# Two-layer hybrid decoder: the row sums of the later modulation vectors by 32x32 turns on VectorE, their running sums pinned in program order

## The chip, the core and the metric

One of the cores of a Trainium2 chip runs the whole program; the other cores have no part in it. The metric is the device time of one execution in microseconds (us). Each kernel is run several times; one further execution is taken by the hardware profiler, and all views of the profile are of that one execution. In the profile PE is TensorE (PEld its weight loads), DVE is VectorE, ACT is ScalarE, POOL is GpSimd, and SP issues most of the transfers. L391 is line 391 of the kernel.

## What is computed

The reference is a decoder trunk of two layers over 512 positions and 2048 features, in float32. Layer 0 is differential attention, layer 1 is forgetting attention that reads keys and values shared from the output of layer 0. Ahead of each layer, and of the shared keys and values, the input is scaled and shifted by vectors that come from the conditioning `c`; the mixer's output is multiplied by a third such vector.

```python
c_act = jax.nn.silu(c)
for l in range(DEPTH):
    mod = c_act @ w_mod[l] + b_mod[l]
    shift, scale, gate = jnp.split(mod, 3, axis=-1)
    h = x * (1.0 + scale[:, None]) + shift[:, None]
    ...
    x = layer_norm(DN_ALPHA * x + gate[:, None] * y, ln_g[l], ln_b[l])
...
mod = c_act @ w_mod_kv + b_mod_kv
shift, scale = jnp.split(mod, 2, axis=-1)
hk = x * (1.0 + scale[:, None]) + shift[:, None]
```

So eight vectors of 2048 elements are needed, each one row `c_act` times a 2048x2048 matrix plus a bias. Two of them (shift and scale of layer 0) are needed before anything else. The other six, the later modulation, are what the change is about: the gate of layer 0, shift and scale of the shared keys and values, and shift, scale and gate of layer 1.

## The kernel before

**Large products.** Every projection is a product of 512 positions with a weight matrix, in float32 precision from three products in the faster type float32r: each operand is split into a high part (a copy on ScalarE) and a low part (a subtraction on VectorE), and `products` (L171) issues high*high, high*low and low*high, each 128x128 by 128x512. A weight matrix streams through `WeightStream`: a stage `wst` of two 128x512 tiles is loaded on the SP queue, `whi` is cast on ScalarE (L93) and `wlo` subtracted on VectorE (L94), three of each ahead at most. `group` (L306) runs the eight stages of one job over four accumulators, one burst of six products for each stage and accumulator. After each burst `tick` (L290) issues at most one waiting piece of attention from the list `pieces` and a number `bg` of background steps.

**Order of the jobs.** A hand-written start computes the first projections of heads 0 and 1. Then follow the query-key and value-gate groups of heads 2 to 7, with the attention of the head before (`attention_a`, L683) spread over them as pieces, then the output projection of layer 0 in four jobs (`out_projection`, L884), the shared values and keys (four groups each), eight groups of layer 1 with its attention, and its output projection.

**The later modulation before.** `mod_stream` (L355) is a generator of background steps. For each of 24 segments (a vector's 512 columns) it takes the 16 row blocks of the matrix: it loads them (tile `ms`, 512 KB with two row blocks in stage A, 256 KB with one in stage B, where the first 64 go to free tiles `msk`), and each step adds one block, times the column of `cact` that belongs to it, to a 128x512 accumulator `macc` (L389 for the first block, L391 for the rest). Stage A has 16 segments (256 steps) and two `ms` tiles; its steps are issued by the groups of heads 3 to 7 (45 steps a head) and by the first job of the output projection (one after each of its 32 bursts). Stage B has eight segments (128 steps) during the groups of shared values and keys.

What is left of a segment is a sum over the 128 partitions. `mod_row` (L401) does it on TensorE: `macc` is split into `mhi` and `mlo` (L168, L169), two products with a matrix of ones (L411, L412) give 128 equal rows of sums in the one bank `tr`, which attention's turns use as well; VectorE adds the bias to one of these rows (L413, tile `mrow`), and the row goes to a DRAM row that later stages read (`gate_dram`, `mod_dram`). The first half is issued with step 1 of the next segment, the second with step 5.

**Who reads the results.** `out_projection` broadcasts the gate row. `open_n` (L913), called by the evacuation of the first accumulator in the first job of the output projection, runs out the background, then `fold` (L931) brings the shift and scale of the shared keys and values into columns by one turn on TensorE (L934); only behind it, on VectorE, come the evacuations of that job (`ztmp`, L899). Another `fold`, for layer 1, stands in the third group of shared keys.

**What sets the order.** Each engine runs its own instructions strictly in the order in which they stand. That order is made when the program is built: a scheduler takes instructions by priority and by its own idea of when inputs are there, so a step whose inputs it takes for ready can stand earlier on VectorE than where the program issued it. Only the start's VectorE work is kept as written. In the program before, 240 VectorE instructions stand ahead of the first query split of head 2, and 12 of them are running sums of the modulation.

Of the kernel before, what the change touches and what calls it, by code (L numbers as in the profile page):

```python
# [2 lines left out]

# [6 lines left out]
F32 = mybir.dt.float32  # L10
F32R = mybir.dt.float32r
I32 = mybir.dt.int32
AF = mybir.ActivationFunctionType
ALU = mybir.AluOpType

P = 128
D = 2048
# [92 lines left out]
def tile_yoco(  # L110
# [23 lines left out]
    nc = tc.nc  # L134
    V, S, PE, G = nc.vector, nc.scalar, nc.tensor, nc.gpsimd
# [6 lines left out]
    const = ctx.enter_context(tc.tile_pool(name="const", bufs=1))  # L142
# [12 lines left out]
    def acc_bank(name="acc"):  # L155
        return ps.tile([P, 512], F32, name=name, tag="acc", bufs=4)
# [4 lines left out]
    def tr_bank(name="tr"):  # L161
        return ps.tile([P, 512], F32, name=name, tag="tr", bufs=1)
# [4 lines left out]
    def split(hi, lo, src):  # L167
        S.copy(hi, src)  # L168
        V.tensor_tensor(lo, src, hi.bitcast(F32), op=ALU.subtract)  # L169
# [8 lines left out]
    ident = const.tile([P, P], F32, name="ident")  # L178
    make_identity(nc, ident)
    ones = const.tile([P, P], F32, name="ones")  # L180
    G.memset(ones, 1.0)
    mask = const.tile([P, 512], F32, name="mask")
    G.memset(mask, 0.0)
    G.affine_select(
# [14 lines left out]
    pt = tr_bank()  # L199
    PE.transpose(pt[:, 0:KT], crow, ident[0:KT, 0:KT])  # L200
    V.tensor_copy(ccol, pt[:, 0:KT])
    cact = const.tile([P, KT], F32, name="cact")
# [4 lines left out]
    pt = tr_bank()  # L207
# [147 lines left out]
    def mod_stream(segs, new_stage, new_acc, nk, deep=0, new_deep=None):  # L355

        todo = [(i, r) for i in range(len(segs)) for r in range(KT // nk)]
        loaded = {}  # L360
        summed = []

        def load(k):
            i, r = todo[k]
            src, col, _ = segs[i]
            t = new_deep() if k < deep else new_stage()
            rows = src[nk * r * P : nk * (r + 1) * P, col : col + 512]
            nc.sync.dma_start(t, rows.rearrange("(k p) n -> p k n", p=P) if nk > 1 else rows)
            loaded[k] = t

        def load_upto(k):
            n = len(loads)
            while n < len(todo) and n <= (k + 7 if n < deep else k + 2 // nk):
                load(n)
                loads.append(n)
                n += 1

        loads = []
        load_upto(-1)
        for k, (i, r) in enumerate(todo):  # L380
            load_upto(k)
            if r == 0:
                acc = new_acc()
            t = loaded.pop(k)
            for kk in range(nk):
                kt = nk * r + kk
                w = t[:, kk, :] if nk > 1 else t
                if kt == 0:
                    V.tensor_scalar(acc, w, cact[:, 0:1], None, op0=ALU.mult)  # L389
                else:  # L390
                    V.scalar_tensor_tensor(acc, w, cact[:, kt : kt + 1], acc, op0=ALU.mult, op1=ALU.add)  # L391
                if kt == KT - 1:
                    summed.append(segs[i][2](acc))
                if kt in (1, 5) and summed:
                    if next(summed[0], None) is None:
                        summed.pop()
                yield
        for _ in summed[0]:
            yield

    def mod_row(pool, ones_r, dst, bias, one):  # L401

        def steps(acc):
            hi = pool.tile([P, 512], F32R, name="mhi", tag="mhi", bufs=1)
            lo = pool.tile([P, 512], F32R, name="mlo", tag="mlo", bufs=1)
            split(hi, lo, acc)
            row = pool.tile([1, 512], F32, name="mrow", tag="mrow", bufs=1)
            nc.sync.dma_start(row, bias.rearrange("(o n) -> o n", o=1))
            yield True
            pt = tr_bank()  # L410
            PE.matmul(pt, ones_r, hi, start=True, stop=False)  # L411
            PE.matmul(pt, ones_r, lo, start=False, stop=True)  # L412
            V.scalar_tensor_tensor(row, pt[0:1, :], one, row, op0=ALU.add, op1=ALU.add)  # L413
            nc.sync.dma_start(dst, row)
        return steps


# [4 lines left out]
    with tc.tile_pool(name="start", bufs=2, reuse_waits="tile") as sp, tc.manual_schedule(engines={ET.DVE}):  # L422
# [44 lines left out]
        def mod_steps():  # L467
            for n, (i, k, nr) in enumerate(tiles):
                k0, nk = sets[i]
                load_mods(n + NBUF)  # L470
                if k >= KT - on_pe(i):
                    continue
                if k == 0:
                    accs[i] = sp.tile([P, 2, 2 * P], F32, name="sacc", tag="sacc", bufs=2)
                acc = accs[i][:, :, : nk * P]
                for kq in range(nr):
                    w, sc = loaded[i, k][:, kq, :, :], cact[:, k + kq : k + kq + 1]
                    if k + kq == 0:
                        V.tensor_scalar(acc, w, sc, None, op0=ALU.mult)
                    else:  # L480
                        V.scalar_tensor_tensor(acc, w, sc, acc, op0=ALU.mult, op1=ALU.add)  # L481
                    yield i
# [3 lines left out]
        steps = mod_steps()  # L486
# [46 lines left out]
        acc = {}  # L533
# [96 lines left out]
    actx = ExitStack()  # L630
    ap = actx.enter_context(tc.tile_pool(name="ap", bufs=1, reuse_waits="tile"))
    segs = []
    ones_a = ap.tile([P, P], F32R, name="ones_a")
    S.copy(ones_a, ones)
    for dst, src, col, bias, one in (
        (gate_dram[0], w_mod[0], 2 * D, b_mod[0], 0.0),
        (mod_dram[0][0:1, :], kv_w_mod, 0, kv_b_mod, 0.0),
        (mod_dram[0][1:2, :], kv_w_mod, D, kv_b_mod, 1.0),
        (mod_dram[1][0:1, :], w_mod[1], 0, b_mod[1], 0.0),
    ):  # L640
        for f0 in range(0, D, 512):
            cs = slice(col + f0, col + f0 + 512)
            segs.append((src, col + f0, mod_row(ap, ones_a, dst[:, f0 : f0 + 512], bias[cs], one)))
    background = mod_stream(
        segs,
        lambda: ap.tile([P, 2, 512], F32, name="ms", tag="ms", bufs=2),
# [342 lines left out]
    npool, n, nstats = zp  # L989
# [81 lines left out]
    acc = [acc_bank() for _ in range(TB)]  # L1071
    held = {}
    for i, (half, s) in enumerate(lag):
# [7 lines left out]
        hi, lo = held[s]  # L1081
        for b in (2 * half, 2 * half + 1):
            bs = slice(b * P, (b + 1) * P)
            for kq in range(2):
                kt = 2 * s + kq
# [4 lines left out]
            ws.advance(ws.where[id(vj[0]), s] + 4)  # L1090
    forget = [forget_logits(q) for q in range(4)] + [None, forget_sums] + [None] * 8 + [columns_of_f]
    pieces.extend(forget)
    ones_b = npool.tile([P, P], F32R, name="ones_b")
    S.copy(ones_b, ones)
    segs = []
    for dst, col, one in ((mod_dram[1][1:2, :], D, 1.0), (gate_dram[1], 2 * D, 0.0)):
        for f0 in range(0, D, 512):
            cs = slice(col + f0, col + f0 + 512)
            segs.append((w_mod[1], col + f0, mod_row(npool, ones_b, dst[:, f0 : f0 + 512], b_mod[1, cs], one)))
    background = mod_stream(  # L1100
        segs,
        lambda: npool.tile([P, 512], F32, name="ms", tag="ms", bufs=3),
# [243 lines left out]
```

## Time and profile before

| what | value |
|---|---|
| median of 3 runs | 2009.19 us (2004.58 to 2010.02) |
| the profiled execution, device time | 2010.56 us |
| its span (first to last instruction) | 2008.7 us, granted TensorE clock 0.995 |
| ScalarE, VectorE, GpSimd: busy share of the span | 36%, 66%, 0% |
| bytes moved by transfers, mean rate | 353.79 MB, 176 GB/s |
| running sums L391, all forms | 360 instructions, 0.75 us each |

The profiled execution is 1.4 us above the median, inside the spread of the three runs. Busy time of PE is the time in which at least one matmul is under way; matmuls overlap, so the time that a further matmul costs is the distance between starts and not its duration.

### The profile page before, as it was taken

To read this page: it belongs to the slowest core of one execution; us is meant where nothing else is said; L and a number is where in the kernel's file an instruction comes from. 1 tells how busy PE (TensorE), PEld (TensorE's weight loads), DVE (VectorE), ACT (ScalarE), POOL (GpSimd) and SP (SyncE) were. 2 spreads that over 40 slices of the span, in tenths; PEclk is the share of its full clock that TensorE was granted. 3 is DMA by queue.
4 is the path that set the end of the run, shared out by engine and by line. 5 is a ranking of instruction groups with operands and counts; after the bars stand their busy time and mean duration, and the time that the engine had idled before them with its cause. 6 is when DMAs were issued, how large, how long until landed. Compare 5 with 4: busy or idle time off the path is not lost.

```text
span 2008.7 us, 25012 instructions
## 1 busy us (share of the span) xinstructions
PE 1964.6 (98%) x9115; PEld 1627.1 (81%) x9115; DVE 1335.3 (66%) x2436; ACT 725.6 (36%) x1235; POOL 2.2 (0%) x10
## 2 busy tenths in 40 slices
PE   5999999999999999999999999999999999999996
PEld 4888878888888888788888888888888888888885
DVE  6887865677777777853576666635455555576578
ACT  2432445333333334431263222224343434353232
POOL 0000000000000000000000000000000000000000
PEclk8999999999999999999999999999999999999998
DMA  9994742375757676452346787634323232333664
GB/s 338 348 314 147 237 157 78 111 228 182 226 182 229 191 223 209 161 166 95 118 144 223 234 275 260 224 95 131 100 90 105 95 105 90 104 123 104 215 210 178
DMA packets 263095, 353.79 MB, mean 176 GB/s; under 512 B 18022, under 2 KB 162556, under 8 KB 262204
## 3 DMA queue, kind: packets, MB, share of 16 engines
q1 hardware_dynamic: 260592, 347.99, 53.2%
q10 hardware_dynamic: 2380, 4.21, 0.6%
q8 instruction: 71, 1.16, 0.2%
q14 instruction: 52, 0.43, 0.1%
HBM read 339.47 MB, written 12.66 MB: 175 GB/s over the span
## 4 chain that ended last, share of the span: by engine, by line
PE 87%; DVE 6%; DMA 4%; issue 1%; SPq 1%; ACT 0%; DVEq 0%; ACTq 0%
PE acc L173 25%; PE acc L174 25%; PE acc L175 25%; DMA ms<-in_w_mod_dram 3%; PE sc L173 2%; PE sc L174 2%; PE sc L175 2%; DVE wlo L94 1%; PE o L175 1%; PE o L173 1%; PE o L174 1%; DVE macc L391 1%; PE tr L1203 1%; DMA sms<-in_w_mod_dram 1%; SPq L454 0%
## 5 line engine op out<-in xcount | busy, mean ns | idle before, releaser
L94 DVE TENSOR_TENSOR wlo<-wst,whi 128x1024 fp32r<-128x1024 f32 (+2 forms) x338 | 403.4, 1196 | 278.9 <-ACT whi L93 276.9
L93 ACT CAST whi<-wst 128x1024 fp32r<-128x1024 f32 (+2 forms) x338 | 348.5, 1032 | 640.8 <-PE acc L175 327.5
L173 PE MATMUL acc<-whi,hh 128*128 128x512 f32 x1244 | 488.6, 396 | 1.7 <-DVE sg L680 1.7
L174 PE MATMUL acc<-wlo,hh 128*128 128x512 f32 x1244 | 485.3, 390 | 0.8 <-DVE wlo L94 0.8
L175 PE MATMUL acc<-whi,hl 128*128 128x512 f32 x1244 | 485.0, 390 | 0.0
L173 PE MATMUL acc<-hh,whi 128*128 128x512 f32 x1184 | 470.4, 397 | 0.9 <-DVE part L561 0.5
L174 PE MATMUL acc<-hl,whi 128*128 128x512 f32 x1184 | 462.3, 390 | 0.0
L175 PE MATMUL acc<-hh,wlo 128*128 128x512 f32 x1184 | 462.2, 390 | 0.0
L391 DVE SCALAR_TENSOR_TENSOR macc<-ms,cact,macc 128x512 f32<-128x512 f32 x300 | 224.9, 750 | 86.1 <-DMA ms<-in_w_mod_dram 59.4
L173 PEld LDWEIGHTS acc<-whi,hh 128*128 128x128 f32 x1244 | 234.9, 189 | 49.0 <-PE acc L175 1.4
L175 PEld LDWEIGHTS acc<-whi,hl 128*128 128x128 f32 x1244 | 233.6, 188 | 50.0
L174 PEld LDWEIGHTS acc<-wlo,hh 128*128 128x128 f32 x1244 | 233.8, 188 | 46.7 <-DVE wlo L94 1.2
L175 PEld LDWEIGHTS acc<-hh,wlo 128*128 128x128 f32 x1184 | 222.3, 188 | 48.6
L173 PEld LDWEIGHTS acc<-hh,whi 128*128 128x128 f32 x1184 | 222.6, 188 | 43.5 <-issue 0.9
L174 PEld LDWEIGHTS acc<-hl,whi 128*128 128x128 f32 x1184 | 222.8, 188 | 39.3
L481 DVE SCALAR_TENSOR_TENSOR sacc<-sms,cact,sacc 128x512 f32<-128x512 f32 (+1 forms) x127 | 89.5, 705 | 6.1 <-DMA sms<-in_w_mod_dram 2.4
L710 ACT ACTIVATE e<-e,mn 128x128 f32<-128x128 f32 (+3 forms) x64 | 36.1, 564 | 126.4 <-DVE mn L706 126.2
L1192 ACT ACTIVATE eb<-eb,mnb 128x128 f32<-128x128 f32 (+1 forms) x64 | 36.1, 564 | 95.5 <-DVE mnb L1189 94.4
L1189 DVE CUSTOM_DVE_ANT_0 eb<-sc,biasb 128x128 f32<-128x128 f32 (+1 forms) x64 | 31.4, 490 | 55.4 <-PE sc L175 55.4
L391 DVE SCALAR_TENSOR_TENSOR macc<-msk,cact,macc 128x512 f32<-128x512 f32 x60 | 44.5, 749 | 14.7 <-DMA msk<-in_w_mod_dram 13.6
L1207 DVE TENSOR_TENSOR pTl<-tr,pTh 128x128 fp32r<-128x128 f32 (+1 forms) x64 | 31.2, 487 | 25.2 <-ACT pTh L1206 24.7
L706 DVE CUSTOM_DVE_ANT_0 e<-sc,bias 128x128 f32<-128x128 f32 (+3 forms) x64 | 31.1, 486 | 20.9 <-PE sc L175 20.9
(259 smaller groups left out, 1776.5 us busy)
## 6 DMA issues: line engine op xcount, KB each, us to landing
wst<-in_a_w_in_dram SPq DMA_DIRECT2D x240, 256.0 KB
ms<-in_w_mod_dram SPq DMA_DIRECT2D x64, 512.0 KB
ms<-in_kv_w_mod_dram SPq DMA_DIRECT2D x64, 512.0 KB
wst<-in_kv_w_dram SPq DMA_DIRECT2D x64, 512.0 KB
wst<-in_b_w_in_dram SPq DMA_DIRECT2D x128, 256.0 KB
sms<-in_w_mod_dram SPq DMA_DIRECT2D x56, 512.0 KB
wst<-in_b_w_out_dram SPq DMA_DIRECT2D x48, 512.0 KB
wst<-in_a_w_out_dram SPq DMA_DIRECT2D x32, 512.0 KB
```

The lines of the kernel that those rows point to most:

```text
L93: self.nc.scalar.copy(hi[:, :, :w], st[:, :, :w])
L94: self.nc.vector.tensor_tensor(lo[:, :, :w], st[:, :, :w], hi[:, :, :w].bitcast(F32), op=ALU.subtract)
L173: PE.matmul(dst, lhs[0], rhs[0], start=start, stop=False)
L174: PE.matmul(dst, lhs[0], rhs[1], start=False, stop=False)
L175: PE.matmul(dst, lhs[1], rhs[0], start=False, stop=stop)
L391: V.scalar_tensor_tensor(acc, w, cact[:, kt : kt + 1], acc, op0=ALU.mult, op1=ALU.add)
L481: V.scalar_tensor_tensor(acc, w, sc, acc, op0=ALU.mult, op1=ALU.add)
L706: V.tensor_tensor_reduce(out=e[:, :w], in0=sc[:, :w], in1=st["bias"][:, (3 - i) * P :], scale=-1.0, scalar=3.0e38, op0=ALU.add, op1=ALU.mi ...
L710: S.activation(e[:, :w], e[:, :w], AF.Exp, bias=mn, scale=-1.0, accum_out=rs)
L1189: V.tensor_tensor_reduce(out=e[:, :w], in0=sc[:, :w], in1=bias[:, :w], scale=-1.0, scalar=3.0e38, op0=ALU.add, op1=ALU.min, accum_out=mn)
L1192: S.activation(e[:, :w], e[:, :w], AF.Exp, bias=mn, scale=-1.0, accum_out=rs)
L1207: V.tensor_tensor(pTl[:, 0 : i + 1, ts], src, pTh[:, 0 : i + 1, ts].bitcast(F32), op=ALU.subtract)
```

## The change

Four edits.

1. `mod_row` becomes `mod_rows`, one for each vector of 2048 and not for each segment. For each segment VectorE turns `macc` in blocks of 32x32 (`mturn`), and adds up runs of 32 elements, which gives 16 columns of the tile `mred`; after four segments `mred` is 128x64. One product with `fours` (four 32x32 identities on top of each other) adds the four groups of 32 partitions and leaves the vector as 64 rows of 32. The bias is loaded in that shape, added, and the vector written in one transfer.
2. `fours` is built by four small copies on GpSimd at the start; the float32r matrices of ones, `ones_a` and `ones_b`, go.
3. Each running sum is given to `tc.keep_in_program_order`: it may not stand ahead of the VectorE instruction that was issued last before it.
4. The callers make four segments from one `mod_rows`.

```diff
+    fours = const.tile([P, 32], F32, name="fours")
+    for k in range(0, P, 32):
+        G.tensor_copy(fours[k : k + 32, :], ident[k : k + 32, k : k + 32])
...
                 if kt == 0:
-                    V.tensor_scalar(acc, w, cact[:, 0:1], None, op0=ALU.mult)
+                    ins = V.tensor_scalar(acc, w, cact[:, 0:1], None, op0=ALU.mult)
                 else:
-                    V.scalar_tensor_tensor(acc, w, cact[:, kt : kt + 1], acc, op0=ALU.mult, op1=ALU.add)
+                    ins = V.scalar_tensor_tensor(acc, w, cact[:, kt : kt + 1], acc, op0=ALU.mult, op1=ALU.add)
+                tc.keep_in_program_order(ins)
...
-    def mod_row(pool, ones_r, dst, bias, one):
-        def steps(acc):
-            hi = pool.tile([P, 512], F32R, name="mhi", tag="mhi", bufs=1)
-            lo = pool.tile([P, 512], F32R, name="mlo", tag="mlo", bufs=1)
-            split(hi, lo, acc)
-            row = pool.tile([1, 512], F32, name="mrow", tag="mrow", bufs=1)
-            nc.sync.dma_start(row, bias.rearrange("(o n) -> o n", o=1))
+    def mod_rows(pool, dst, bias, one):
+        red = []
+        def steps(n, acc):
+            if n == 0:
+                red.append(pool.tile([P, 64], F32, name="mred", tag="mred", bufs=2))
+            t = pool.tile([P, 512], F32, name="mturn", tag="mturn", bufs=1)
+            V.transpose(t, acc)
+            V.tensor_reduce(
+                red[0][:, 16 * n : 16 * n + 16], t.rearrange("p (j q) -> p j q", q=32), axis=mybir.AxisListType.X, op=ALU.add
+            )
+            if n == 3:
+                row = pool.tile([64, 32], F32, name="mrow", tag="mrow", bufs=1)
+                nc.sync.dma_start(row, bias.rearrange("(j q) -> j q", q=32))
             yield True
-            pt = tr_bank()
-            PE.matmul(pt, ones_r, hi, start=True, stop=False)
-            PE.matmul(pt, ones_r, lo, start=False, stop=True)
-            V.scalar_tensor_tensor(row, pt[0:1, :], one, row, op0=ALU.add, op1=ALU.add)
-            nc.sync.dma_start(dst, row)
+            if n == 3:
+                pt = tr_bank()
+                PE.matmul(pt[0:64, 0:32], red[0], fours, start=True, stop=True)
+                V.scalar_tensor_tensor(row, pt[0:64, 0:32], one, row, op0=ALU.add, op1=ALU.add)
+                nc.sync.dma_start(dst.rearrange("o (j q) -> (o j) q", q=32), row)
         return steps
...
-        for f0 in range(0, D, 512):
-            cs = slice(col + f0, col + f0 + 512)
-            segs.append((src, col + f0, mod_row(ap, ones_a, dst[:, f0 : f0 + 512], bias[cs], one)))
+        steps = mod_rows(ap, dst, bias[col : col + D], one)
+        segs += [(src, col + 512 * f, partial(steps, f)) for f in range(4)]
```

In the order in which the built program's instructions stand, TensorE keeps its sequence but for the products that go and come and a few neighbours that change places. On VectorE the first running sum moves from place 205 to place 390, and the sums then stand where the background issues them: 45 for each of heads 3 to 7, and the rest in the first job of layer 0's output projection. Between the last gate evacuation of head 7 (L680) and the first `ztmp` stand 32 running sums, where 3 stood before.

More of the change, by code (lines that the diff above doesn't have):

```diff
@@ L2 @@
 from contextlib import ExitStack
+from functools import partial
 import concourse.bass as bass
@@ L632, in tile_yoco @@
     segs = []
-    ones_a = ap.tile([P, P], F32R, name="ones_a")
-    S.copy(ones_a, ones)
     for dst, src, col, bias, one in (
@@ L1092, in tile_yoco @@
     pieces.extend(forget)
-    ones_b = npool.tile([P, P], F32R, name="ones_b")
-    S.copy(ones_b, ones)
     segs = []
     for dst, col, one in ((mod_dram[1][1:2, :], D, 1.0), (gate_dram[1], 2 * D, 0.0)):
-        for f0 in range(0, D, 512):
-            cs = slice(col + f0, col + f0 + 512)
-            segs.append((w_mod[1], col + f0, mod_row(npool, ones_b, dst[:, f0 : f0 + 512], b_mod[1, cs], one)))
+        steps = mod_rows(npool, dst, b_mod[1, col : col + D], one)
+        segs += [(w_mod[1], col + 512 * f, partial(steps, f)) for f in range(4)]
     background = mod_stream(
```

## The prediction

> **What bounds the kernel now.** I read the page first, then PE's idle time, then stretches of the span, then single instructions.
>
> ```profile
> PE 1964.6 (98%) x9115; PEld 1627.1 (81%) x9115; DVE 1335.3 (66%) x2436; ACT 725.6 (36%) x1235; POOL 2.2 (0%) x10
> ```
>
> TensorE is never without work but for 44 us, most of it in the first 50 us and in the tail. All the 24 row sums lie between 389 and 1358 us, in stages that PE fills. So a product that goes shortens the span by the distance between two starts. That distance is read from starts, here around one row sum:
>
> ```profile
> 869.03 0.39 PE L411 MATMUL tr<-mhi,ones_a 128*128 128x512 f32 x1
> 869.27 0.39 PE L412 MATMUL tr<-mlo,ones_a 128*128 128x512 f32 x1
> 869.50 0.39 PE L173 MATMUL acc<-whi,hh 128*128 128x512 f32 x1
> ```
>
> A pair holds PE for 869.50 - 869.03 = 0.47 us, though each product lasts 0.39. Next, PE's waits between 200 and 350 us, and between them the chain of work that ended last:
>
> ```profile
> PE tr L774 <- DVE og L760: 2.7, 3, 1.3
> PE o L175 <- DVE al L169: 0.6, 1, 0.6
> PE acc L173 <- DVE part L561: 0.5, 1, 0.5
> ```
> ```profile
> 194.48 4.63 DMA ms<-in_w_mod_dram
> 199.21 0.76 DVE macc L391
> ...
> 200.66 0.69 DVE wlo L94
> 201.35 0.61 DVE part L561
> ```
>
> The second shows why: a running sum placed early waits for its 512 KB, VectorE stands still behind it, and the evacuation that PE needs comes late. Last, VectorE itself, in the last third of head 7 and in the first job of the output projection (columns: stretch, length, busy us and instructions of PE, PEld, DVE, ACT, POOL, granted clock, DMA share, GB/s), and in the second stretch the `macc` instructions alone (DVE, ACT):
>
> ```profile
> 778.00:833.00 55.00, 53.98 (x254) 44.30 (x252) 46.43 (x79) 26.21 (x49) 0.00 (x0) 1.00 0.74 241
> 832.00:883.50 51.50, 50.86 (x252) 42.11 (x251) 32.04 (x90) 22.12 (x50) 0.00 (x0) 1.00 0.40 133
> ```
> ```profile
> 832.00:883.50 51.50, 3.58 (x5) 1.24 (x2) 1.00 0.40 133
> ```
>
> In the first, VectorE is busy 84% with waits for modulation tiles in between; in the second it is only 62% busy, since the running sums are nearly done.
>
> **The change, part by part.**
>
> *Products that go.* 24 pairs by 0.47 us = 11.2 us. Three of them (838.8, 869.0 and 880.9 us) lie in the stage that I take apart below; the other 21 give 9.8 us. Cover: none, PE is the bound there.
>
> *Products that come.* Six, 64 rows by 32 columns in plain float32, not in the trace. The nearest is the small turn that follows in `fold`:
>
> ```profile
> 882.87 0.24 PE L934 MATMUL tr<-ident,mrow 32*128 32x32 f32 x1
> 883.04 0.50 PE L173 MATMUL acc<-whi,hh 128*128 128x512 f32 x1
> ```
>
> 883.04 - 882.87 = 0.17 us. Lower bound 0.1, upper a whole pair, 0.47; I take 0.2, so 1.0 us for the five outside that stage. Net so far 8.8 us (bounds 7.5 to 9.3).
>
> *VectorE's part of the row sums.* 24 subtractions (L169, 0.67 us) and 24 bias sums (L413, 0.68 us) go, 32.4 us; 24 turns and 24 sums over runs of 32 come, and six small bias sums. Neither is in the trace. One pass over 128x512 costs 0.49 us at the cheapest (L389), 0.68 for the statistics, which also read 512 and write few (L901, 885.93 us); a turn in two passes would be 1.35. I take 0.67 each, 32.2 us: no difference in sum, -9 to +16 us at the bounds, spread over 66%-busy VectorE, so it costs only in the stage below. The Trainium skill (VectorE: DVE Perf Modes, Rules for kernel authors) speaks against this edit: it expects the reduction at its slowest mode on a hot path and advises restructuring; by that the edit costs VectorE time, while the statistics row at 0.68 says that it replaces work of the same size. No run here shows the reduction yet.
>
> *ScalarE.* 24 casts (L168, 0.62 us) go, 15 us of an engine 36% busy, and with them the 21.3 us in which ScalarE stood at L168 until L411's product let `mhi` go. I count nothing: PE's own waits name ScalarE nowhere after 100 us. Four POOL copies at the start feed a product first needed after 400 us: nothing. On the SP queue 48 transfers of 2 KB become 12 of 8 KB in pieces of 128 bytes; a vector's row now leaves after its fourth segment, but each reader comes later still (the gate row is read at 880 us, its segments end before 450). Nothing, and 36 fewer places where SP stands until `mrow` is written (29.8 us in 20 waits now, hidden by stages loaded three ahead).
>
> *The early sums move back.* About 58 sums that ran between 177 and 400 us, with their 29 transfers of 512 KB on the SP queue, now start at about 320 us. The waits of PE at 201, 258 and 275 us stand behind such sums; measured as starts further apart than 0.23 they cost 0.65 + 1.43 + 1.11 = 3.2 us. The third wait for `og` (335 us) has no sum ahead of it and stays. Between nothing and 3.2; I take 2.5. Heads 4 to 7 get 45 sums where 48 ran, so they stay as they are.
>
> *The late sums land in the first output job.* 32 sums stand between the last gate evacuation and the first `ztmp`, with three turns and three reductions. VectorE's work from 832 us to that `ztmp`: 32.04 - 3.58 (old `macc`) - 2.02 (old `mrow`) + 32 x 0.75 + 6 x 0.67 = 54.5 us, where 51.5 were there. Behind the last reduction stand the small product, the bias sum, the turn of `fold`, three small sums and `ztmp`: from the bias sum (881.99) to `ztmp` (883.53) pass 1.5 us now, and with the product and its hand-over I take 2.3. Against this PE has 3.6 us more than before, since its order now puts the small product at the job's end (887.1 us is when the next job started), and VectorE enters 2 us earlier, with three sums fewer in the stretch before. With VectorE never waiting, the job ends 54.5 + 2.3 - 51.5 - 3.6 - 2.0 = -0.3 us late, that is, on time. At the 84% of the stretch before, 54.5 becomes 64.9 and it ends 10 us late. I take 92% (the waits fall away in part, as VectorE is behind and tiles land meanwhile): 59.2, 4.4 us late; and 1.5 us for a PE that starts again slowly (the rows are with the rivals). Sum 6, bounds 0 to 13. Queued behind those sums on VectorE are the low halves of the weights, the attention of head 7 and the evacuations; PE waits for all three.
>
> *Stage B.* The last two groups of keys (1293 to 1382 us, VectorE busy 42 of 89) get some 40 sums, 30 us: it fits. If it did not, PE would wait for `wlo` there.
>
> **The sum.** -8.8 - 2.5 + 6 = -5.3 us. Against the profiled execution (2010.56 us, span 2008.7) that is 2005.3; it ran 1.4 above the median, so against the median 2009.2 - 5.3 = 2003.9, I say 2004. The measurement can tell about 0.3%, 6 us, from no change, and the forecast lies just within that.
>
> **Rivals.**
>
> *All of it arrives* (22%). VectorE fits the 32 sums in, the early waits go whole: 8.8 + 1.3 for the three pairs + 3.2 = 13 us, 1996. For it: the 0.3 us of the ledger, and waits of VectorE that exist only because it was early. Against: the stretch before, with the same density, had 7.5 us of such waits in eight sums.
>
> *The first output job becomes VectorE's* (slower, 18%). Two `ms` tiles let a load start only when the sum two tiles back is done, and landings of 4 to 6 us then set the pace. If VectorE manages 78% it needs 69.9 us, 15 late; PE idles in pieces and then runs its first products at half speed:
>
> ```profile
> 35.28 0.63 PE L173 MATMUL o<-hh,whi 128*128 128x512 f32 x1
> 35.70 0.63 PE L173 MATMUL acc<-whi,hh 128*128 128x512 f32 x1
> ...
> 38.22 0.40 PE L174 MATMUL acc<-wlo,hh 128*128 128x512 f32 x1
> 38.46 0.39 PE L175 MATMUL acc<-whi,hl 128*128 128x512 f32 x1
> ```
>
> Starts 0.42 apart, then 0.24; eight such cost about 1.5 us, twice 3. With the early gain at 1: -8.8 - 1 + 15 + 3 = +8, 2017. It decides from about 10 us late, which is VectorE below 84% or turns of 1.35. The Trainium skill (TensorE: Matmul & The Clock Gate, Part 1) has the clock halved after an idle window of about 3.4 us; by that only a wait in one piece would add this, and the rows after 34 us agree in the half speed.
>
> *It does not pay* (13%). The removed products were slots in which VectorE caught up, and PE waits for `wlo` and evacuations instead: 2009, within 3. For it: heads 4 to 7 keep VectorE at 74 to 82%. Against: only 2 us of PE waits there now.
>
> **Chances and range.** Forecast 47%, its own range 1999 to 2009; under half of it lies below 2003. Faster by over 0.3%: 22 + 20 = 42%. Within: 27 + 13 = 40%. Slower: 18%. The range reaches from a little below the full gain to where the slower rival begins: 1994 to 2014.
>
> **What would show it.** No L411/L412 rows, six small products about 0.2 us apart from the next start; turns and reductions near 0.67 us; no PE wait at 201, 258 and 275; VectorE over 90% busy between the last gate evacuation and the first `ztmp`, and a PE wait of some us at that job's end. I am wrong if that wait is missing or over 10 us, or if heads 4 to 7 show new PE waits.

## The result, and the profile after

| kernel | median us | runs | lowest to highest |
|---|---|---|---|
| before | 2007.38 | 5 | 2004.58 to 2010.02 |
| changed | 2020.38 | 5 | 2016.89 to 2020.79 |

The changed kernel takes 1.0059 times as long, interval 1.0048 to 1.0070: about 12 us more, where 5 less were forecast. Its profiled execution took 2016.89 us (span 2015.1), the lowest of its five, 3.5 below their median, while that of the kernel before was 3.2 above the median in this table. So the two profiles lie 6.4 us apart where the medians lie 13, and the views below can explain no more than these 6.4.

The busy times of the page hardly differ from those before, so they tell little:

```profile
PE 1957.9 (97%) x9079; PEld 1619.5 (80%) x9079; DVE 1339.3 (66%) x2442; ACT 711.1 (35%) x1209; POOL 2.9 (0%) x14
```

TensorE has 36 products fewer (48 went, and the six small float32 products are recorded as 12), is busy 6.7 us less, and the span is 6.4 us longer: 13 us of new waiting. First its waits between 200 and 350 us, then, from its waits in the whole execution, the long ones behind the start:

```profile
PE tr L787 <- DVE og L773: 0.5, 1, 0.5
```
```profile
...
PE tr L428 <- DVE mred L419: 8.6, 1, 8.6
...
PE tr L787 <- DVE al L170: 1.8, 1, 1.8
...
PE acc L174 <- DVE ztmp L912: 1.2, 1, 1.2
```

The early waits at 201, 258 and 275 us are gone; only the one for `og` at 335 us is left, as the prediction had it. In their place stands one wait of 8.6 us, and two small ones in the same stage, for attention's `al` and for `ztmp`. The long one is that of the small product (L428) at the end of the first output job. TensorE's own rows there:

```profile
882.00 0.39 PE L176 MATMUL acc<-whi,hl 128*128 128x512 f32 x1
890.95 0.42 PE L428 MATMUL tr<-fours,mred 128*64 128x32 f32 x2 [8.56 <-DVE mred L419]
891.65 0.31 PE L947 MATMUL tr<-ident,mrow 32*128 32x32 f32 x1 [0.28 <-DVE mrow L429]
893.11 0.80 PE L174 MATMUL acc<-whi,hh 128*128 128x512 f32 x1 [1.16 <-DVE ztmp L912]
893.71 0.63 PE L175 MATMUL acc<-wlo,hh 128*128 128x512 f32 x1
894.13 0.63 PE L176 MATMUL acc<-whi,hl 128*128 128x512 f32 x1
```

The last product of the job starts at 882.00, the first of the next at 893.11, and the next ones follow at 0.43 us and not at 0.23. What led up to it stands in the chain of work that ended last (start, length, what):

```profile
866.94 5.54 DMA ms<-in_w_mod_dram
...
872.57 0.75 DVE macc L397
873.32 1.13 DVE wlo L95
874.45 0.67 DVE macc L397
875.12 0.02 issue
875.14 5.89 DMA ms<-in_w_mod_dram
...
881.12 0.76 DVE macc L397
...
881.91 0.76 DVE macc L397
...
882.69 4.75 DMA ms<-in_w_mod_dram
...
889.46 0.72 DVE mturn L418
...
890.21 0.70 DVE mred L419
```

Two running sums, a landing of 4.75 to 5.89 us, two running sums again. After the last landing come two sums, the turn and the reduction, and only then the product. VectorE from the end of the last gate evacuation to the first `ztmp`, before and after (stretch, length, busy us and instructions of PE, PEld, DVE, ACT, POOL, granted clock, DMA share, GB/s):

```profile
833.84:883.53 49.69, 49.69 (x245) 41.20 (x245) 30.23 (x87) 21.74 (x49) 0.00 (x0) 1.00 0.39 128
```
```profile
829.03:892.38 63.35, 51.33 (x250) 41.55 (x248) 51.31 (x119) 21.20 (x48) 0.00 (x0) 0.95 0.74 241
```

VectorE has 51.3 us of work where it had 30.2, and spreads it over 63.35 us: 81% busy, not the 92% of the forecast. The work itself is no more than the 54.5 us that the forecast had; the error is in the waits, 12 us. TensorE, busy throughout before, stands 12 us. The clock is granted at 0.95 in that stretch.

The span can be cut at four instructions that every kernel has: the first gate evacuation of all (L693), the first one of head 7, the first `ztmp` of the second output job, the first `ztmp` of layer 1's output projection. The column "stage B" is all that lies between the last two, the shared values and keys and layer 1 among it. In us, each kernel's profiled execution, those of the experiments below too:

| kernel | start | heads | first output job | stage B | rest |
|---|---|---|---|---|---|
| before | 209.4 | 619.6 | 97.4 | 931.4 | 150.9 |
| changed | 211.9 | 611.7 | 111.9 | 928.3 | 151.2 |
| b_pinonly | 207.5 | 618.3 | 112.5 | 931.5 | 151.0 |
| a_nopin | 211.8 | 630.0 | 96.7 | 932.8 | 152.3 |
| c_ms3 | 213.9 | 609.2 | 104.2 | 929.2 | 151.6 |
| j_noload | 213.3 | 613.4 | 103.4 | 928.6 | 151.2 |
| d_early | 214.2 | 611.2 | 96.4 | 929.0 | 151.5 |
| g_shift | 212.5 | 618.5 | 97.4 | 931.0 | 151.0 |
| e_pad | 206.9 | 612.3 | 111.6 | 929.1 | 151.3 |
| f_early_pad | 206.7 | 611.3 | 96.5 | 929.6 | 151.7 |
| i_old_early | 207.7 | 618.4 | 96.5 | 931.4 | 151.0 |
| l_off0 | 206.8 | 611.8 | 96.4 | 929.2 | 151.2 |
| m_off128 | 212.4 | 611.8 | 96.4 | 928.8 | 151.3 |
| k_best | 207.0 | 610.2 | 96.0 | 929.1 | 151.2 |

The first two rows say: heads 7.9 us shorter and stage B 3.1, as forecast; the first output job 14.5 longer; and a start that should not differ at all, 2.5 longer. Each row is one execution, so a difference of one or two us between two rows shows little by itself.

### The profile page after: what moved, and what is told of

Read it like the earlier page. It is cut to its first block, busy times and chain, and to the rows that moved or that the text cites. A ratio compares the mean times of both kernels' runs of the same rounds, so it can differ in the third digit from the quotient of the medians.

```text
span 2015.1 us, 24837 instructions
## 1 busy us (share of the span) xinstructions
PE 1957.9 (97%) x9079; PEld 1619.5 (80%) x9079; DVE 1339.3 (66%) x2442; ACT 711.1 (35%) x1209; POOL 2.9 (0%) x14
## 4 chain that ended last, share of the span: by engine, by line
PE 85%; DVE 6%; DMA 6%; SPq 1%; issue 1%; ACT 1%; DVEq 0%; ACTq 0%
PE acc L174 25%; PE acc L176 25%; PE acc L175 25%; DMA ms<-in_w_mod_dram 3%; PE sc L174 2%; PE sc L176 2%; PE sc L175 2%; DMA sms<-in_w_mod_dram 1%; DVE macc L397 1%; PE o L176 1%; PE o L175 1%; PE o L174 1%; DVE wlo L95 1%; PE tr L1213 1%; SPq L470 1%
```

## The experiments

### One part alone

**a_nopin**: the new row sums, without the pinning.

```diff
-                tc.keep_in_program_order(ins)
```

> The changed kernel without the pinning: the row sums by turns stay, the running sums may again stand early, none of them between the last gate evacuation of head 7 and the first ztmp. Theory T (the pinned sums in the first output job are what costs, with landings of 4 to 6 us setting their pace; the new row sums pay): the wait of about 9 us for the small product at the job's end is gone, the removed products give some 8 to 11 us, the early waits near 201 and 258 us come back; 1996 to 2001. Rival R1 (the new row sums themselves cost, by turns, reductions and the way through the small product): 2012 or more, with waits of PE for them wherever a vector ends. Rival R2 (the pinning makes VectorE's order worse everywhere): also about 1997, but then heads 2 to 7 must be shorter here than in the changed kernel, while T has them about 3 us longer.

Measured: 2025.63 us, 1.0082 (1.0066 to 1.0097) of the kernel before. T and R2 missed it; the time is in R1's range, but R1's sign is missing, since hardly any wait of TensorE stands at a row sum (0.9 us in all). The job's wait is gone (96.7 us), as T says, but the heads took 630.0 us, 18 more than in the changed kernel. The `macc` instructions of VectorE between 250 and 550 us, in the kernel before and in this one (stretch, length, busy us and instructions, clock, DMA share, GB/s; the kernel before has an ACT column too):

```profile
250.00:350.00 100.00, 10.49 (x14) 0.00 (x0) 1.00 0.37 117
350.00:450.00 100.00, 24.79 (x34) 1.24 (x2) 1.00 0.53 167
450.00:550.00 100.00, 36.13 (x50) 1.86 (x3) 1.00 0.65 205
```
```profile
250.00:350.00 100.00, 39.70 (x55) 1.00 0.67 211
350.00:450.00 100.00, 44.79 (x62) 0.98 0.74 231
450.00:550.00 100.00, 44.00 (x61) 1.00 0.73 231
```

178 such instructions run there instead of 98. With the old row sums the scheduler had spread the stream; with the new ones, unpinned, it puts the stream ahead of its time (why, no run shows), and VectorE stands behind landings, by its own waits between 250 and 600 us, 36.9 us in these two rows where the kernel before has 18.5:

```profile
DVE macc L397 <- DMA ms<-in_kv_w_mod_dram: 24.6, 24, 3.1
DVE macc L397 <- DMA ms<-in_w_mod_dram: 12.3, 15, 2.0
```

Evacuations stand behind these sums on VectorE, and TensorE waits for `og`, `sg` and `q0l` (12.0 us between 250 and 600 us). So the pinning is no mere loss: it keeps the new row sums out of this order.

**b_pinonly**: the kernel before, with the pinning and the old row sums.

```diff
-                    V.tensor_scalar(acc, w, cact[:, 0:1], None, op0=ALU.mult)
+                    ins = V.tensor_scalar(acc, w, cact[:, 0:1], None, op0=ALU.mult)
...
+                tc.keep_in_program_order(ins)
```

> The kernel before with the pinning alone: the old row sums by two products with ones. 32 running sums stand between the last gate evacuation and the first ztmp. Theory T: the job's end comes some 14 us later as in the changed kernel, the early waits give about 3 us back, no product is saved; 2016 to 2024. Rival R1 (the row sums cost, not the pinning): 2002 to 2009. A wait of 5 us or more of PE for the last row sum (its product L411) near 890 us is there by T and missing by R1.

Measured: 2022.26 us, 1.0071 (1.0056 to 1.0086). TensorE's longest wait after the start (the line numbers are one higher than in the kernel before):

```profile
PE tr L412 <- ACT mhi L168: 7.5, 1, 7.5
```

The same place, now the last old row sum. Theory T holds, R1 is out: the job takes 112.5 us with the old row sums and 111.9 with the new. The heads gain 1.3 us from the pinning. By the ratios the new row sums alone cost 16 us, about 5 of them by an address that is told below, and the pinning alone 14; both together cost 12. They do not add up: without the pinning the scheduler gives the new row sums another order of running sums than the old ones had.

### What paces the first output job

**c_ms3**: the changed kernel with three tiles `ms` in stage A.

```diff
-        lambda: ap.tile([P, 2, 512], F32, name="ms", tag="ms", bufs=2),
+        lambda: ap.tile([P, 2, 512], F32, name="ms", tag="ms", bufs=3),
```

> The changed kernel with three instead of two tiles ms for the modulation rows of stage A: a load may start one tile earlier. Theory T with landings as the pace: VectorE's waits for ms between 828 and 892 us fall from 13 us to below 5, the PE wait for the last reduction from 8.6 to under 4, the time to 2008 to 2014. Rival R3 (VectorE's own work is the pace, the landings only fill its gaps): the wait of PE stays at 7 to 9 us and the time within 3 us of the changed kernel's, about 2020. Rival R4 (the transfers together are the limit, so a third tile only moves the wait, with weights landing later): waits for ms fall, but wlo or wst land later and PE waits there.

Measured: 2009.7 us, 1.0007 (0.9998 to 1.0017). VectorE's waits for `ms` in the changed kernel, and here (stretches 829 to 893 and 828 to 885 us):

```profile
DVE macc L397 <- DMA ms<-in_w_mod_dram: 8.5, 10, 1.6
```
```profile
DVE macc L397 <- DMA ms<-in_w_mod_dram: 1.9, 2, 1.7
```

The wait of TensorE for the last reduction falls from 8.6 to 3.5 us, the job from 111.9 to 104.2, and no wait for weights takes its place (R4). So the landings set part of the pace, as T says; but 7 us over the kernel before remain (104.2 against 97.4).

**j_noload**: the changed kernel with the last 32 running sums of stage A on a tile that is already there. It leaves out 16 transfers of 512 KB, so its last modulation vector comes from other numbers; VectorE's instructions all stay.

```diff
+            if not deep and k >= 112:
+                loaded[k] = kept[0]
+                return
```

> The changed kernel, but the last 32 running sums of stage A, those that land in the first output job, read the last loaded tile again instead of loading their own (16 transfers of 512 KB left out, so that the last modulation vector is not the reference's; all instructions of VectorE stay). Rival R3 (VectorE's own work is the pace of that job): the wait for the last reduction stays at 6 us or more, the job from the last gate evacuation to the second accumulator job's first ztmp stays at 108 to 112 us. Theory T (the landings are the pace): the wait falls under 1 us and the job takes 97 to 99 us as in the kernel before; 2005 to 2009. With three tiles the job took 104 us, so a result between, 100 to 104, would say that work of VectorE sets the last 3 to 7 us.

Measured: 2009.59 us, 1.0017 (1.0008 to 1.0026). The stretch from the last gate evacuation to the first `ztmp`:

```profile
832.08:886.10 54.02, 50.76 (x250) 41.65 (x248) 50.75 (x119) 21.15 (x48) 0.00 (x0) 1.00 0.37 126
```

With no transfer to wait for, VectorE is 94% busy and still needs 54.0 us, where the kernel before took 49.7. The job takes 103.4 us. So of the 14.5 us, about 8.5 go with the transfers (111.9 - 103.4), and 6 stay without them (103.4 - 97.4), 4.3 of these in VectorE's stretch (54.02 - 49.69). T and R3 each hold for one part, as the expectation had it for a result between. The third tile of c_ms3 came within 1 us of this (104.2) with all transfers running, so it is the two tiles that cost most of the 8.5, and not the amount that is moved.

**d_early**: the changed kernel, with the background begun one head earlier.

```diff
-    group(qk[2], False, lambda b, acc: keep(("qk", b), acc))
+    group(qk[2], False, lambda b, acc: keep(("qk", b), acc), bg=lambda k: k % 2)
...
-    group(vg[2], True, keep_vg)
+    group(vg[2], True, keep_vg, bg=lambda k: k % 2)
```

> The changed kernel with pinning kept, but the background begins in head 2 instead of head 3, so that the stream of running sums is through before the first output job, which gets none. Theory T: the wait at that job's end goes whole (about 14 us), the saved products stay; if VectorE has room in head 2, 1996 to 2003, the best of these four. Against: if the sums in head 2 make evacuations late, PE waits of 1 to 3 us show between 210 and 310 us. Rival R1: no better than 2012.

Measured: 2003.23 us, 0.9973 (0.9964 to 0.9983). The stream is through before the job; this takes 96.4 us, 1 less than before, and the waits feared in head 2 are not there (heads 611.2). T holds, with the time at the upper end of what was expected. But its start took 214.2 us, and by the table the starts fall into two sets.

### Why the start is longer

In the start TensorE waits for the running sums of the first two vectors, and these wait for transfers. The stretch from 20 to 60 us in the kernel before and in the changed one:

```profile
20.00:60.00 40.00, 34.86 (x155) 28.31 (x155) 34.24 (x52) 11.43 (x17) 0.00 (x0) 0.87 1.09 380
```
```profile
20.00:60.00 40.00, 32.80 (x145) 26.58 (x145) 32.25 (x48) 10.57 (x17) 0.00 (x0) 0.83 1.11 345
```

The transfer engines are busy throughout in both (DMA share over 1), with the same instructions queued, but they move 345 GB/s instead of 380. What differs is an address: `fours` takes 128 bytes of each partition ahead of nearly all other buffers. In the built programs the tiles `sms`, `wst` and `xt` start at 256 within 512 bytes before, and at 384 after.

**g_shift**: the kernel before with an unused tile of 128 bytes in that place.

```diff
+    gap = const.tile([P, 32], F32, name="gap")
+    G.memset(gap, 0.0)
```

> The kernel before with one unused tile of 128 bytes (set to zero by GpSimd once) where the changed kernel has fours: all buffers behind it stand 128 bytes further on; no other edit. Theory A: the rate between 20 and 60 us falls to about 348 GB/s, the start ends 3 to 5 us later, 2010.5 to 2013. Rival A1: no change, 2008 within 1.5.

Measured: 2012.19 us, 1.0019 (1.0010 to 1.0028), 3.9 us over the kernel before. Theory A, by which those 128 bytes of address slow the transfers of the start, holds:

```profile
20.00:60.00 40.00, 33.34 (x145) 27.04 (x146) 32.16 (x48) 10.51 (x17) 0.00 (x0) 0.87 1.11 345
```

**e_pad**: the changed kernel with the tile 512 bytes wide.

```diff
-    fours = const.tile([P, 32], F32, name="fours")
+    fours = const.tile([P, 128], F32, name="fours")[:, 0:32]
```

> The changed kernel with the tile fours laid 512 bytes wide in each partition instead of 128 (the product still uses 32 columns). Nothing else moves but addresses: with 128 bytes every buffer behind fours stands 128 bytes further on, with 512 they stand at the same place within 512 bytes as in the kernel before. Theory A (in the stage of the start, which waits for transfers, those 128 bytes cost: between 20 and 60 us transfers moved about 385 GB/s in the kernel before and in the one that only pins, about 348 in all four that have the 128-byte tile): the rate goes back to 375 or more, the start's end (first gate evacuation) to 208 to 210 us, the time falls by 2 to 5, to 2015 to 2018. Rival A1 (the start differs by the four copies on GpSimd or by chance): rate and time stay, 2020.

Measured: 2015.81 us, 1.0034 (1.0021 to 1.0046), against 1.0059 for the changed kernel: 383 GB/s, start 206.9 us. The first output job still takes 111.6.

**l_off0** and **m_off128**: both mends (early background, wider `fours`), but `fours` 256 or 384 bytes wide, so that the buffers behind start at 0 or 128 within 512.

```diff
-    fours = const.tile([P, 128], F32, name="fours")[:, 0:32]
+    fours = const.tile([P, 64], F32, name="fours")[:, 0:32]
```

> The kernel with both mends, but fours 256 bytes wide: all buffers behind it start at 0 within 512 bytes (in the kernel before at 256, in the changed one at 384). Theory A in the form that a multiple of 256 bytes is what counts: rate at the start 380 GB/s or more, 1997. Theory A in the form that the place within 512 bytes matters otherwise: another rate, above 390 or below 370, and 1 us or more of difference.

> The same with fours 384 bytes wide: all buffers behind it start at 128 within 512 bytes. If a multiple of 256 is what counts: 348 GB/s at the start and 2001 to 2004, as with 384. If only the place 384 is bad, 380 GB/s and 1997.

Measured: 1997.49 us, 0.9957 (0.9943 to 0.9970), and 2001.78 us, 0.9976 (0.9966 to 0.9985). First 0, then 128:

```profile
20.00:60.00 40.00, 35.57 (x167) 29.16 (x166) 34.78 (x52) 12.06 (x18) 0.00 (x0) 0.87 1.09 383
```
```profile
20.00:60.00 40.00, 31.91 (x140) 25.65 (x139) 31.12 (x47) 9.26 (x15) 0.00 (x0) 0.83 1.11 345
```

Of the four places tried, 0 and 256 give 380 to 383 GB/s, 128 and 384 give 345. Among these four a multiple of 256 bytes is what counts. The seven starts at 0 or 256 took 206.7 to 209.4 us (mean 207.4), the seven others 211.8 to 214.2 (mean 212.9): 5.4 us.

### What the row sums are worth, and the best version

**f_early_pad**: the changed kernel with the early background and the 512-byte `fours` (the diffs of d_early and e_pad together).

> Both mends together: the background begins in head 2 (no running sum in the first output job), and fours is laid 512 bytes wide. By theory A 1997 to 2001, 3 to 5 below the kernel that only begins early; by A1 the same as that one, 2003. By theory T with the prediction's terms for the products it should beat the kernel before by about 8 to 10 us.

Measured: 1996.96 us, 0.9943 (0.9930 to 0.9955): 11 us below the kernel before. The first output job is TensorE's again, VectorE 57% busy:

```profile
823.46:870.63 47.17, 47.17 (x236) 38.93 (x235) 26.98 (x82) 20.98 (x48) 0.00 (x0) 1.00 0.42 131
```

**i_old_early**: b_pinonly with the early background, so the old row sums under the same order.

```diff
+    group(qk[2], False, lambda b, acc: keep(("qk", b), acc), bg=lambda k: k % 2)
...
+    group(vg[2], True, keep_vg, bg=lambda k: k % 2)
```

> The kernel before with pinning, and the background begun in head 2, but with the old row sums by products with ones (and so without the 128-byte tile). No running sum stands in the first output job. It isolates what the row-sum form is worth when that job is clear: against the kernel with both mends this one has 24 pairs of products more. If the prediction's 0.47 us for a pair and 0.2 for a small product hold, it is 8 to 11 us slower than that kernel, 2006 to 2010; if the new row sums are worth nothing or cost, it is at 2001 or below.

Measured: 2006.61 us, 0.9990 (0.9981 to 0.9999). Against f_early_pad the old row sums cost 2006.61 - 1996.96 = 9.7 us, 7.1 of it in the heads and 1.8 in stage B. With the job clear, the new form of the row sums is worth what the prediction said.

**k_best**: f_early_pad with three tiles `ms`.

```diff
-        lambda: ap.tile([P, 2, 512], F32, name="ms", tag="ms", bufs=2),
+        lambda: ap.tile([P, 2, 512], F32, name="ms", tag="ms", bufs=3),
```

> The kernel with both mends (background begun in head 2, fours 512 bytes wide) and three tiles ms. With three tiles heads 2 to 7 were 2 to 3 us shorter than with two, beside the gain in the first output job. Theory: the same 2 us here and nothing in the job, which is clear already: 1994 to 1996. Rival: no gain, 1997, since the sums no longer press.

Measured: 1994.95 us, 0.9942 (0.9930 to 0.9955) against a kernel before of 2006.93 in the same set: 12 us below it and, by the ratios, 0.0117 or 23 us below the changed kernel. Beside f_early_pad (0.9943) the ratios show no gain; the heads are 1.1 us shorter in the two profiles. Whether the third tile still helps is open.

## Why the prediction was wrong

**Products that go and come: right.** Forecast: 10.1 us, 8.8 outside the first output job and 1.3 in it. Measured: 9.7, with the job clear. The small product is recorded as two of 0.08 and 0.15 us between starts, 0.23 together against the 0.2 assumed.

**VectorE's part of the row sums: right.** Both new operations against 0.67 us forecast (count, then shortest, median and longest in ns):

```profile
L418 DVE STREAM_TRANSPOSE mturn<-macc x24: 702/710/714, 377.4 to 1362.1; 128x512 f32<-128x512 f32 x24
```
```profile
L419 DVE TENSOR_REDUCE mred<-mturn x24: 667/684/689, 378.7 to 1363.1; 128x16 f32<-128x512 f32 x24
```

Each takes about as long as the subtraction and the bias sum that they replace (0.67 and 0.68). The Trainium skill (VectorE: DVE Perf Modes, Rules for kernel authors) spoke against the reduction on a hot path, as the slowest operation of VectorE. The trace does not agree: its 0.684 us are less than the 0.75 of a running sum and the 0.710 of the turn.

**ScalarE, POOL, SP: "nothing" was wrong, and this is the term that was missing.** The four copies on GpSimd cost nothing, as said. The tile that they fill moves the buffers of the start (`sms`, `wst`, `xt`) by 128 bytes, and that costs 5.4 us by the starts, and 3.8 to 6.0 by the ratios of four pairs (before and g_shift, e_pad and changed, f_early_pad and d_early, l_off0 and m_off128). The prediction looked at the instructions of the diff, and not at where the tiles lie.

**The early sums move back: right in kind, half in size.** The waits went as forecast; the pinning alone is worth 1.3 us in the heads, forecast 2.5, bounds 0 to 3.2. But the comparison was with an order that the new row sums would not have had: without the pinning the heads take 18 us more than with it (a_nopin against the changed kernel).

**The late sums in the first output job: the mechanism was right, the term mis-sized: +6 forecast, +14.5 measured, bounds 0 to 13.** Three places of its working failed.

- The stretch on VectorE. Forecast: 54.5 us of work at 92% plus 2.3 for the way to `ztmp`, against 51.5 before, so 10.0 longer. Measured: 63.35 against 49.69, 13.7 longer. The work was not too low (51.3 us busy, where the forecast counted 54.5 from 832 us on); the waits made it long. They did not "fall away in part": with two tiles a load cannot start before the sums two tiles back are done, so a VectorE that is behind makes its transfers late too, and stays at 81%.
- The 3.6 us allowed for TensorE, which had more work left behind the fold than in the kernel before. The kernel before had by count some 12 products of the job left behind the fold (2.7 us from 883.04, so that its next job began near 885.8 and not at 887.1), the changed one has done them by then; but it then waits 1.2 us for `ztmp`, which frees the accumulator. 1.5 us are left of the 3.6.
- The 2.0 us for VectorE's earlier entry. It does not enter earlier as TensorE sees it: the gate evacuations wait for TensorE's products, and end 0.6 us later after the first of them than before.

The slow restart cost 1.8 us (eight starts), where 1.5 were forecast. In sum 13.7 + 0.6 - 2.7 + 1.2 + 1.8 = 14.6, against 14.5 in the table. The prediction's own sign, a wait at the job's end that is missing or over 10 us, did not show, with 8.6 us in that wait: the other waits and the restart came on top. The ledger behind "that is, on time" fell as well: with no landing to wait for the job is 6 us late, not 0.3 early (j_noload).

**Stage B fits: right.** 928.3 to 929.6 us with the new row sums pinned (932.8 unpinned), 931.0 to 931.5 with the old.

So the slower rival was the nearest one: two `ms` tiles, landings of 4 to 6 us, a job about 15 us late, 2017. It was given 18%, below the forecast, because a share of VectorE had to be chosen between 78 and 92% and the favourable end was taken. With the address on top, the changed kernel lies beyond that rival. Of the 13 us between the medians, the table of stages places 6.4, and the mean starts (5.4 instead of 2.5) another 2.9; where the rest lies, no profile shows.

## What to carry to other kernels

When a change moves work into a stage, the share of its engine there must come from who sets the pace of its inputs, not from how busy it would like to be; with two buffers a late consumer makes its own producer late. A new constant tile is an address change for everything allocated behind it: look at the built addresses, and keep what transfers fill at multiples of 256 bytes, which were the fast places here. Two edits that both act on a scheduler are tried apart and together, since each alone can be worse than both.

## What the runs showed of the hardware

**A transfer's rate hangs on where its tile starts.** 380 to 383 GB/s at multiples of 256 bytes against 345 at the two odd multiples of 128, the transfer engines busy in both. The single packets in the traces show it too: between 20 and 60 us one of 1024 bytes took 46 ns in the kernel before and 52 in the changed one, one of 512 bytes 27 and 32, so about 5 ns more at either length. Time is lost where transfers are the pace: TensorE's products in the changed kernel run 4.3 us behind those of e_pad by 48 us, 5.1 by 85 us, and 5.0 still at 192 us. The Trainium skill (DMA: Bandwidth & Descriptors, How a descriptor splits into AXI transactions) says that a piece which does not start at a multiple of 256 bytes is begun at the multiple below, and that the bytes ahead of its start are fetched unused and still cost. By that page an estimate: 128 bytes more on each packet of 955 bytes (the mean of the kernel before in this stretch, 15.21 MB in 15932 packets) makes 380 into 335; the trace agrees in kind, with a smaller loss. The page speaks of reads; here the side that was moved is the one written.

**The slow restart came after several short waits too.** In j_noload TensorE never waits longer than 1.68 us in one piece at the end of the first output job:

```profile
882.14 0.39 PE L176 MATMUL acc<-whi,hl 128*128 128x512 f32 x1
884.21 0.30 PE L433 MATMUL tr<-fours,mred 128*64 128x32 f32 x2 [1.68 <-DVE mred L424]
885.44 0.24 PE L952 MATMUL tr<-ident,mrow 32*128 32x32 f32 x1 [0.92 <-DVE mrow L434]
886.84 0.80 PE L174 MATMUL acc<-whi,hh 128*128 128x512 f32 x1 [1.16 <-DVE ztmp L917]
887.43 0.63 PE L175 MATMUL acc<-wlo,hh 128*128 128x512 f32 x1
```

Three waits with two small products between them, 3.8 us of waiting in 4.7, and the following products start 0.43 us apart until 892.1 us, twelve of them, where the 8.6 us of the changed kernel were followed by eight. The granted clock says why the longer wait had fewer: it is 0.50 from 885.61 to 892.43 us in j_noload and from 886.59 to 896.83 us in the changed kernel, of which 6.5 us passed while TensorE still waited. The prediction took the idle window of the Trainium skill (TensorE: Matmul & The Clock Gate, Part 1) for one wait in one piece; these rows say that short products inside the gap do not save the clock.
